# A small tile placed elsewhere, two weight splits queued later, three PSUM adds done after the products

## The chip, the core and the metric

The kernel runs on one core of a Trainium2 chip. A core has five engines with a queue each: TensorE (PE in the profile) multiplies matrices and writes to PSUM, VectorE (DVE) and ScalarE (ACT) do elementwise work, GpSimd (POOL) and SyncE (SP) here issue most of the DMAs, and POOL does a little elementwise work. Each engine works off its own queue and waits for the others by semaphores. The metric is device time in microseconds (us) of one execution; lower is better.

## The reference

One layer over 1024 latent tokens of 1024 channels and 256 context tokens, in fp32:

```
hx = rmsnorm(x) * (1 + sc1) + sh1
z  = hx @ w_in                      -> u_pool, u_lru, u_gate, g_pool, g_lru
m  = sigmoid(g_pool) * (pool_mixer(u_pool) @ w_proj_pool)
   + sigmoid(g_lru)  * (((h_f + h_b) * gelu(u_gate)) @ w_proj_lru)   # h_f, h_b: two RG-LRU scans
x  = x + ga1 * rmsnorm(m @ w_out)
h  = rmsnorm(x) * (1 + sc2) + sh2
g, u = split(h @ w_up)              # 3072 channels each
g  = depthwise 3x3 convolution of g over the 16 x 64 grid + bias
x  = x + ga2 * rmsnorm((gelu(g) * u) @ w_down)
```

## The kernel before, in words

**Arithmetic.** Operands of a matmul are fp32r. To keep fp32 accuracy, each operand is split (function `split`, lines 86 to 88) into a high part, a cast on ScalarE in line 87, and a low part, a subtraction on VectorE in line 88; a product is three matmuls, high by high, high by low and low by high. Nearly every matmul is 128x128 weights by 512 moving columns.

**Order of the work.** First the modulation vectors, then the projections of `hx` by `w_in` (lines 231 to 243, function `unit_mm`), with the pooling branch (lines 303 to 384) and the recurrent units (lines 466 to 534), then the two merging projections and `w_out` (line 702, eight token tiles), then the ConvFFN's up projection (lines 771 to 866, 24 tiles of 128 channels, called f) and the down projection (line 915). An operation can be pulled ahead of its place in the code: the scheduler that builds the queues takes what is ready by priority, and `tc.high_priority(offset=n)` moves an instruction n places ahead. `tc.issue_after(i)` puts every instruction of its block behind instruction i in the queue of i's engine. Tiles that share a tag share its buffers: a new tile's first writer waits until all readers of the tile that had the buffer are done, and buffers are handed out in the order of the code.

**Memory.** The pools lie one behind the other: `cpool`, `gpool`, `small`, then `hp` (the tiles `hx`, `hy`, `h2` under one tag) and the pools of the stages. A tile takes a multiple of 32 bytes of each partition. In the built program, `gpool`'s buffers start at multiples of 64 bytes: `raw` at 15296, 19392 and 23488, `whl`, the split weights, at 27584, 35776 and 43968. The last tile of `small` is `s2l`, 8 bytes at 55232, so `hp` starts at 55264, which is 32 modulo 64, and all tiles of `hp` and of the stages' pools that matmuls read (`hx`, `hy`, `yps`, `h2`, `nf`, `wf`, `w22`, `wd`, `gt`) start at 32 modulo 64. So `whl` meets operands at another place, and the others meet operands at their own. In the profile the weights of line 702 and of the recurrent units also bear the name `whl`, but lie in a stage's pool, at 32.

**The ConvFFN up projection.** It computes each tile's two 1024-token halves as a 2x2 block product by seven products of blocks (Winograd's form of Strassen's method) instead of eight. The activation forms are made once. `h2` holds four blocks and two of their differences, made in `h2_tile` (lines 657 to 676) from each token tile's transposes (line 661). `nf` (lines 752 to 765) holds three more forms: N2 is `n2raw`, N3 and N4 are sums of it with blocks of `h2`, made in two tiles `nt` (lines 763 and 764) and split by `nsplit` (lines 754 to 757), each in two halves. The tiles `nt` have the tag `gc` with two buffers, as have the tiles `gc` of the tiles f, which hold the convolution's input in the left half and its result in the right half.

For the first three tiles (f < NPF = 3), the weight forms were made earlier and are loaded from DRAM on POOL's queue, and the two products with the plain weights `whl` were done between the token tiles (loop in lines 740 to 745): one on X (right half of the PSUM tile `XQ`), one on Q (its left half). For f >= 3 `weights(f)` (lines 769 to 792) loads two weight tiles on SP's queue into `raw` (three buffers), splits them (`load_pair`, lines 678 to 684, with priority WPRI = 200) and makes four sums and three more splits on VectorE and ScalarE.

A tile f has `mid` and `tail`. In `mid` (lines 808 to 834), for the first three tiles, the first product on X is saved by `fork` (a copy on ScalarE into a tile `fk`, line 797), the product with N2 is added on X, the one with N3 starts `v`, X is copied again, and line 829 adds the saved product to Q on VectorE. Then come the product with N1 on X and a third copy. For f >= 3 the saved product is copied to Q itself (line 818) and PE adds to it there. In `tail` (lines 836 to 866) X gets the product with B22 and `v` the one with N4; line 843 subtracts, line 845 starts the convolution's result on ScalarE with the middle tap, and eight more taps follow in line 856 on VectorE; GELU is line 864, the product with u line 865, the store line 866 on POOL's queue.

`s2l` itself is used once, in the last row tile of the down projection (function `finish`), for two partial sums of squares.

Of the kernel before, what the change touches and what calls it, by code (L numbers as in the profile page):

```python
# [8 lines left out]
F32 = mybir.dt.float32  # L9
# [8 lines left out]
P = 128  # L18
# [22 lines left out]
def block_kernel(ctx: ExitStack, tc: tile.TileContext, x, cx, vecs, rowv, icnt, w_mod1, w_mod, w_in, pool_w,  # L41
# [41 lines left out]
    def f32(ap):  # L83
        return ap.bitcast(F32)
# [468 lines left out]
    with tc.tile_pool(name="pj", bufs=1, reuse_waits="tile") as zp:  # L553
# [121 lines left out]
            A.copy(hi, n1)  # L675
            V.tensor_sub(lo, n1, f32(hi))

        def load_pair(f):
            ru = gpool.tile([P, 1024], F32, name=uid("raw"), tag="raw", bufs=3)
            nc.sync.dma_start(ru, w_up[NF + f])  # L680
            w = gpool.tile([P, 2, 1024], F32R, name=uid("whl"), tag="whl", bufs=3)
            with tc.high_priority(offset=WPRI):
                split(w[:, 0, :], w[:, 1, :], ru)
            return ru, w

# [63 lines left out]
    with tc.tile_pool(name="ff", bufs=1, reuse_waits="tile") as zp:  # L749
# [3 lines left out]

        def nsplit(q, src):
            for a in range(0, 4, 2):
                A.copy(nf[:, q, a:a + 2, 0, :], src[:, a:a + 2, :])
                V.tensor_sub(nf[:, q, a:a + 2, 1, :], src[:, a:a + 2, :], f32(nf[:, q, a:a + 2, 0, :]))  # L757

        nsplit(0, n2raw)
        for q, o in ((1, 0), (2, 4)):  # L760
            t = zp.tile([P, 4, 512], F32, name=uid("nt"), tag="gc", bufs=2)
            for a in range(0, 4, 2):
                V.tensor_add(t[:, a:a + 2, :], n2raw[:, a:a + 2, :], f32(h2[:, 0, o + a:o + a + 2, 0, :]))  # L763
                V.tensor_add(t[:, a:a + 2, :], t[:, a:a + 2, :], f32(h2[:, 0, o + a:o + a + 2, 1, :]))  # L764
            nsplit(q, t)

        pairs = {}

        def weights(f):
            w22 = zp.tile([P, 2, 512], F32R, name=uid("w22"), tag="w22", bufs=2)  # L770
            w2 = zp.tile([P, 2, 1024], F32R, name=uid("wf"), tag="wf", bufs=3)
            w3 = zp.tile([P, 2, 1024], F32R, name=uid("wf"), tag="wf", bufs=3)
            L, R = slice(0, 512), slice(512, 1024)
            if f < NPF:
                w1 = wu[f][1]
                G.dma_start(w3, wf_d[f, 1])
                G.dma_start(w2, wf_d[f, 0])
                G.dma_start(w22, w22_d[f])
                pairs[f] = (lh(w1, 0), lh(w1, 1), lh(w22, 0), lh(w2, 1), lh(w3, 0), lh(w2, 0), lh(w3, 1))
                return  # L780
            ru, w1 = load_pair(f)
            rg = gpool.tile([P, 1024], F32, name=uid("raw"), tag="raw", bufs=3)
            nc.sync.dma_start(rg, w_up[f])
            with tc.high_priority(offset=WPRI):
                split(w22[:, 0, :], w22[:, 1, :], rg[:, R])
                V.tensor_add(rg[:, R], rg[:, L], rg[:, R])
                V.tensor_add(rg[:, L], rg[:, L], ru[:, L])
                V.tensor_add(ru[:, L], ru[:, L], rg[:, R])
                V.tensor_add(ru[:, R], ru[:, R], ru[:, L])
                split(w2[:, 0, :], w2[:, 1, :], rg)  # L790
                split(w3[:, 0, :], w3[:, 1, :], ru)
            pairs[f] = (lh(w1, 0), lh(w1, 1), lh(w22, 0), lh(w2, 1), lh(w3, 0), lh(w2, 0), lh(w3, 1))

        def fork(src):
            t = zp.tile([P, 512], F32, name=uid("fk"), tag="fk", bufs=3)
            with tc.high_priority(offset=FPRI):
                A.copy(t, src)  # L797
            return t
# [9 lines left out]
        def mid(f):  # L808
            a11, a12, a22, s1, s2, s3, s4 = pairs[f]
            xq, v = XQ[f % 3], Vps[:, (f % 2) * 512:(f % 2 + 1) * 512]  # L810
            X, Q = xq[:, 512:1024], xq[:, 0:512]
            gc = zp.tile([P, 2, SEQ], F32, name=uid("gc"), tag="gc", bufs=2)
            first = f < NPF
            if first:
                p1 = fork(X)
            else:
                with tc.high_priority(offset=FPRI):
                    A.copy(Q, X)
            if f == 0:
                prod(X, s2, N2, False)  # L820
                prod(v, s3, N3, True)
            else:
                prod(v, s3, N3, True)
                prod(X, s2, N2, False)
            u2 = fork(X)
            if not first:
                prod(Q, a12, B21, False)
            if first:
                V.tensor_add(Q, Q, p1)  # L829
            prod(X, s1, N1, False)  # L830
            u4 = fork(X)
            with tc.high_priority(offset=FPRI):
                V.tensor_sub(gc[:, 0, 512:1024], v, u4)
            st[f] = (gc, u2)

        def tail(f):
# [4 lines left out]
            prod(v, a22, N4, False)  # L841
            with tc.high_priority(offset=FPRI):
                V.tensor_sub(gc[:, 0, 0:512], v, u2)
            cw = lambda i, j: vcol("ffn_conv_w", (i * 3 + j) * NF + f)
            A.activation(gc[:, 1, :], gc[:, 0, :], AF.Identity, scale=cw(1, 1), bias=vcol("ffn_conv_b", f))  # L845
            gv = gc[:, 0, :].rearrange("p (r w) -> p r w", w=COLS)
# [48 lines left out]
    with tc.tile_pool(name="dn", bufs=1, reuse_waits="tile") as zp:  # L895
# [23 lines left out]
        def finish(h, t):  # L919
# [5 lines left out]
            ss = small.tile([P, 1], F32, name=uid("ss"), tag="ss1", bufs=3)  # L925
            n = 512 if tt == 7 else D
            if tt == 7:
                s2 = small.tile([P, 2], F32, name="s2l", tag="s2l")
                for c in range(2):
                    o = slice(c * 512, (c + 1) * 512)  # L930
                    A.activation(jk[:, o], psd[t][:, o], AF.Square, accum_out=s2[:, c:c + 1])
# [99 lines left out]
```

## Time and profile before

| what | value |
|---|---|
| median of 3 runs | 1673.47 us (1673.36 to 1674.98) |
| the profiled execution, its own time | 1673.71 us |
| its span, first to last instruction | 1671.9 us |
| PE, DVE, ACT, POOL busy | 1612.0, 1161.9, 669.5, 150.4 us |
| mean granted TensorE clock | 0.989 |

The page of the profile gives busy times, the chain of work that ended last and the costliest groups of instructions; the trace can be asked for stretches of time, for lines of the code and for waits. Times of rows count from the span's start. A matmul's length in a row includes the time until its last result is out, some 390 ns, while the next one begins earlier; how fast matmuls follow each other is read from their starts. A wait in brackets is idle time of the engine just before the instruction, and what ended it.

### The profile page before, as it was taken

Reading aid. Unit: us, or ns where it says so; the run is one execution under the profiler, and the core shown is the slowest. Engines: PE = TensorE matmul, PEld = TensorE weight load, DVE = VectorE, ACT = ScalarE, POOL = GpSimd, SP = SyncE. Lnnn points to the kernel's source line nnn. Section 1 sums busy time; section 2 is a strip of 40 time slices with the busy share of each in tenths; the row PEclk is TensorE's granted clock in tenths of the full one; section 3 lists DMA queues with packets and bytes.
Section 4 is the critical chain, followed back from the end, with each engine's and each line's share of the span. In section 5 each row is a group of like instructions: output and inputs, shape, how many; then the busy total and the mean of one; then the engine's idle time right before and its main releaser. Section 6 shows DMA issues by size and latency. Waiting matters only on the chain.

```text
span 1671.9 us, 18190 instructions
## 1 busy us (share of the span) xinstructions
PE 1612.0 (96%) x7120; PEld 1292.9 (77%) x7120; DVE 1161.9 (69%) x1290; ACT 669.5 (40%) x801; POOL 150.4 (9%) x208
## 2 busy tenths in 40 slices
PE   6899999999999999999999699999999998999997
PEld 4588877877778788888788478888888886888886
DVE  7777673787887744355387689999999998436323
ACT  8523322655577543122143233334333343425222
POOL 1300200111112220010111000000000000000000
PEclk9999999999999999999999899999999999999999
DMA  8335354424232285588354322222222225845611
GB/s 314 116 92 169 127 187 140 127 83 151 76 128 89 86 283 173 174 272 275 117 157 168 116 88 79 85 76 88 84 80 79 86 66 193 295 141 188 207 57 51
DMA packets 68980, 232.51 MB, mean 139 GB/s; under 512 B 7607, under 2 KB 7735, under 8 KB 68126
## 3 DMA queue, kind: packets, MB, share of 16 engines
q1 hardware_dynamic: 48830, 161.20, 30.2%
q0 software_dynamic: 20064, 70.15, 11.6%
q8 instruction: 56, 0.92, 0.2%
q14 instruction: 30, 0.25, 0.0%
HBM read 177.30 MB, written 54.02 MB: 138 GB/s over the span
## 4 chain that ended last, share of the span: by engine, by line
PE 41%; DVE 6%; DMA 2%; issue 1%; ACT 1%; DVEq 0%; POOL 0%; ACTq 0%; SPq 0%; POOLq 0%
PE pb L736 10%; PE pb L915 8%; PE pc L736 6%; PE pd L736 5%; PE pb L702 5%; PE pd L915 4%; PE pc L915 4%; DVE gc L856 2%; DMA raw<-in_w_up_dram 1%; DVE wf L88 1%; DVE nf L757 0%; ACT whl L87 0%; DVE gc L865 0%; DVE nt L764 0%; DVE nt L763 0%
## 5 line engine op out<-in xcount | busy, mean ns | idle before, releaser
L241 PE MATMUL pu<-hx,whl 128*128 128x512 f32 x1056 | 270.5, 396 | 1.3 <-DVE whl L88 1.3
L856 DVE SCALAR_TENSOR_TENSOR gc<-gc,vec 128x945 f32<-128x945 f32 (+1 forms) x192 | 234.5, 1221 | 6.5 <-ACT gc L845 2.2
L241 PEld LDWEIGHTS pu<-hx,whl 128*128 128x128 f32 x1056 | 185.8, 188 | 43.6 <-DVE whl L88 1.9
L87 ACT CAST whl<-raw 128x1024 fp32r<-128x1024 f32 (+1 forms) x98 | 99.3, 1014 | 294.7 <-PE pu L241 62.6
L88 DVE TENSOR_TENSOR whl<-raw,whl 128x1024 fp32r<-128x1024 f32 (+1 forms) x98 | 116.9, 1195 | 89.3 <-ACT whl L87 87.4
L915 PE MATMUL pb<-wd,gt 128*128 128x512 f32 x552 | 132.2, 392 | 0.0
L88 DVE TENSOR_TENSOR wd<-rw,wd 128x1024 fp32r<-128x1024 f32 x46 | 56.3, 1223 | 98.0 <-ACT wd L87 98.0
L915 PEld LDWEIGHTS pb<-wd,gt 128*128 128x128 f32 x552 | 104.6, 190 | 21.9
L241 PE MATMUL pg<-hx,whl 128*128 128x512 f32 x480 | 119.0, 400 | 0.0
L241 PEld LDWEIGHTS pg<-hx,whl 128*128 128x128 f32 x480 | 89.3, 190 | 21.1
L736 PE MATMUL pb<-h,wf 128*128 128x512 f32 x384 | 93.1, 391 | 4.3 <-DVE pb L829 3.0
L736 PE MATMUL pb<-h,whl 128*128 128x512 f32 x384 | 96.4, 395 | 0.7 <-ACT fk L797 0.7
L87 ACT CAST wf<-raw 128x1024 fp32r<-128x1024 f32 x42 | 44.0, 1048 | 120.8 <-PE pb L736 77.8
L87 ACT CAST wd<-rw 128x1024 fp32r<-128x1024 f32 x46 | 48.4, 1053 | 109.5 <-PE pc L915 100.8
L241 PE MATMUL pb<-hy,whl 128*128 128x512 f32 x384 | 90.4, 395 | 0.0
L702 PE MATMUL pb<-whl,mH 128*128 128x512 f32 x384 | 89.1, 391 | 0.6 <-ACT mH L696 0.6
L736 PEld LDWEIGHTS pb<-h,wf 128*128 128x128 f32 x384 | 71.5, 188 | 21.6 <-DVE pb L829 3.8
L736 PEld LDWEIGHTS pb<-h,whl 128*128 128x128 f32 x384 | 71.8, 187 | 18.5 <-ACT fk L797 1.4
L241 PEld LDWEIGHTS pb<-hy,whl 128*128 128x128 f32 x384 | 72.0, 187 | 17.6
L702 PEld LDWEIGHTS pb<-whl,mH 128*128 128x128 f32 x384 | 71.5, 188 | 16.3 <-ACT mH L696 1.1
L736 PE MATMUL pc<-nf,wf 128*128 128x512 f32 x288 | 71.7, 396 | 2.1 <-DVE nf L757 2.0
L915 PE MATMUL pd<-wd,gt 128*128 128x512 f32 x276 | 69.4, 392 | 3.8 <-ACT gt L87 3.5
(276 smaller groups left out, 2830.4 us busy)
## 6 DMA issues: line engine op xcount, KB each, us to landing
raw<-in_w_up_dram SPq DMA_DIRECT2D x51, 512.0 KB, 3.6
rw<-in_w_down_dram SPq DMA_DIRECT2D x46, 512.0 KB, 4.6
raw<-in_w_in_dram SPq DMA_DIRECT2D x40, 512.0 KB, 4.6
rawm<-in_w_mod_dram SPq DMA_DIRECT2D x32, 512.0 KB, 4.2
gu_d<-gc POOLq DMA_DIRECT2D x24, 512.0 KB, 2.9
rg<-gu_d SPq DMA_DIRECT2D x46, 256.0 KB, 4.7
w<-in_w_mod_dram SPq DMA_DIRECT2D x16, 512.0 KB, 6.5
sg_d<-sg POOLq DMA_DIRECT2D x16, 512.0 KB, 3.6
```

The source lines that it names most:

```text
L87: A.copy(hi, src)
L88: V.tensor_sub(lo, src, f32(hi))
L241: mm = T.matmul(ps[:, h * 512:(h + 1) * 512], wv[:, wi, k, :], act(h, k, ai), start=st, stop=sp)
L702: mm = T.matmul(ps[:, h * 512:(h + 1) * 512], mh[ai][:, k, :], wo[k][:, wi, h * 512:(h + 1) * 512], start=(k == 0 and i == 0), stop=(k == ...
L736: mm = T.matmul(ps, w(wi, j), b(ai, j), start=(start and j == 0 and i == 0), stop=(j == 3 and i == 2), skip_group_check=True)
L856: V.scalar_tensor_tensor(o, gv[:, r0 + dr:r1 + dr, c0 + dc:c1 + dc], cw(i, j), o, op0=ALU.mult, op1=ALU.add)
L915: T.matmul(psd[t][:, c * 512:(c + 1) * 512], gt[:, ai, t * P:(t + 1) * P], wd[:, wi, c * 512:(c + 1) * 512], start=(f == 0 and i == 0), st ...
```

## The change

`s2l` moves from `small` to the pool of the down projection (named `dn`), and gets 64 bytes. The split in `load_pair` is put behind the last two instructions of the last `nsplit` for f = 3 and f = 4. For the first three tiles the saved product is copied to the right half of `gc` instead of an `fk` tile, and its addition to Q comes after the last product of the tile, just ahead of line 845 (numbers of the kernel before), which overwrites that half.

```diff
--- before.py
+++ after.py
@@ -675,11 +675,14 @@
             A.copy(hi, n1)
             V.tensor_sub(lo, n1, f32(hi))
 
-        def load_pair(f):
+        def load_pair(f, after=()):
             ru = gpool.tile([P, 1024], F32, name=uid("raw"), tag="raw", bufs=3)
             nc.sync.dma_start(ru, w_up[NF + f])
             w = gpool.tile([P, 2, 1024], F32R, name=uid("whl"), tag="whl", bufs=3)
-            with tc.high_priority(offset=WPRI):
+            with ExitStack() as es:
+                for i in after:
+                    es.enter_context(tc.issue_after(i.ins))
+                es.enter_context(tc.high_priority(offset=WPRI))
                 split(w[:, 0, :], w[:, 1, :], ru)
             return ru, w
 
@@ -753,8 +756,9 @@
 
         def nsplit(q, src):
             for a in range(0, 4, 2):
-                A.copy(nf[:, q, a:a + 2, 0, :], src[:, a:a + 2, :])
-                V.tensor_sub(nf[:, q, a:a + 2, 1, :], src[:, a:a + 2, :], f32(nf[:, q, a:a + 2, 0, :]))
+                ca = A.copy(nf[:, q, a:a + 2, 0, :], src[:, a:a + 2, :])
+                cv = V.tensor_sub(nf[:, q, a:a + 2, 1, :], src[:, a:a + 2, :], f32(nf[:, q, a:a + 2, 0, :]))
+            return ca, cv
 
         nsplit(0, n2raw)
         for q, o in ((1, 0), (2, 4)):
@@ -762,7 +766,7 @@
             for a in range(0, 4, 2):
                 V.tensor_add(t[:, a:a + 2, :], n2raw[:, a:a + 2, :], f32(h2[:, 0, o + a:o + a + 2, 0, :]))
                 V.tensor_add(t[:, a:a + 2, :], t[:, a:a + 2, :], f32(h2[:, 0, o + a:o + a + 2, 1, :]))
-            nsplit(q, t)
+            nsp = nsplit(q, t)
 
         pairs = {}
 
@@ -778,7 +782,7 @@
                 G.dma_start(w22, w22_d[f])
                 pairs[f] = (lh(w1, 0), lh(w1, 1), lh(w22, 0), lh(w2, 1), lh(w3, 0), lh(w2, 0), lh(w3, 1))
                 return
-            ru, w1 = load_pair(f)
+            ru, w1 = load_pair(f, nsp if f < NPF + 2 else ())
             rg = gpool.tile([P, 1024], F32, name=uid("raw"), tag="raw", bufs=3)
             nc.sync.dma_start(rg, w_up[f])
             with tc.high_priority(offset=WPRI):
@@ -812,7 +816,8 @@
             gc = zp.tile([P, 2, SEQ], F32, name=uid("gc"), tag="gc", bufs=2)
             first = f < NPF
             if first:
-                p1 = fork(X)
+                with tc.high_priority(offset=FPRI):
+                    A.copy(gc[:, 1, 0:512], X)
             else:
                 with tc.high_priority(offset=FPRI):
                     A.copy(Q, X)
@@ -825,8 +830,6 @@
             u2 = fork(X)
             if not first:
                 prod(Q, a12, B21, False)
-            if first:
-                V.tensor_add(Q, Q, p1)
             prod(X, s1, N1, False)
             u4 = fork(X)
             with tc.high_priority(offset=FPRI):
@@ -841,6 +844,9 @@
             prod(v, a22, N4, False)
             with tc.high_priority(offset=FPRI):
                 V.tensor_sub(gc[:, 0, 0:512], v, u2)
+            if f < NPF:
+                with tc.high_priority(offset=FPRI):
+                    V.tensor_add(xq[:, 0:512], xq[:, 0:512], gc[:, 1, 0:512])
             cw = lambda i, j: vcol("ffn_conv_w", (i * 3 + j) * NF + f)
             A.activation(gc[:, 1, :], gc[:, 0, :], AF.Identity, scale=cw(1, 1), bias=vcol("ffn_conv_b", f))
             gv = gc[:, 0, :].rearrange("p (r w) -> p r w", w=COLS)
@@ -925,7 +931,7 @@
             ss = small.tile([P, 1], F32, name=uid("ss"), tag="ss1", bufs=3)
             n = 512 if tt == 7 else D
             if tt == 7:
-                s2 = small.tile([P, 2], F32, name="s2l", tag="s2l")
+                s2 = zp.tile([P, 16], F32, name="s2l", tag="s2l")
                 for c in range(2):
                     o = slice(c * 512, (c + 1) * 512)
                     A.activation(jk[:, o], psd[t][:, o], AF.Square, accum_out=s2[:, c:c + 1])
```

## Rows read from the trace of the kernel before

**Rows 1.** The page, part 1: busy time and share of the span of each engine.

```profile
PE 1612.0 (96%) x7120; PEld 1292.9 (77%) x7120; DVE 1161.9 (69%) x1290; ACT 669.5 (40%) x801; POOL 150.4 (9%) x208
```

**Rows 2.** Stretches of the span: length, then busy time (instructions) of PE, PEld, DVE, ACT, POOL.

```profile
72.00:366.00 294.00, 293.88 (x1302) 235.55 (x1303) 197.19 (x182) 107.63 (x120) 34.39 (x62) 1.00 0.41 132
366.00:562.00 196.00, 187.16 (x865) 150.56 (x863) 162.37 (x133) 123.63 (x121) 33.19 (x22) 0.97 0.35 112
...
1005.00:1380.00 375.00, 374.92 (x1630) 304.07 (x1629) 359.09 (x368) 144.99 (x175) 10.69 (x20) 1.00 0.25 81
```

**Rows 3.** Three of these stretches, instructions of line 241 alone.

```profile
72.00:366.00 294.00, 245.72 (x1009) 184.42 (x1009) 1.00 0.41 132
366.00:562.00 196.00, 141.45 (x526) 90.13 (x524) 0.97 0.35 112
562.00:805.00 243.00, 241.49 (x1035) 193.92 (x1035) 1.00 0.66 219
```

**Rows 4.** Timeline of PE in the projections: start, length, instruction, count.

```profile
642.15 11.36 PE L241 MATMUL pd<-yps,whl 128*128 128x512 f32 x48
653.35 9.03 PE L241 MATMUL pc<-yps,whl 128*128 128x512 f32 x38
```

**Rows 5.** The chain that ended last, in the down projection: start, length, count.

```profile
1507.99 16.32 PE pb L915 x72
```

**Rows 6.** Timeline of PE, first matmuls of the down projection.

```profile
1396.74 2.96 PE L915 MATMUL pb<-whl,w 128*128 128x512 f32 x12
1399.54 1.56 PE L915 MATMUL pc<-whl,w 128*128 128x512 f32 x6
```

**Rows 7.** Groups of instructions: shapes, count, busy time, mean ns, idle before.

```profile
L241 PE MATMUL pb<-hy,whl 128*128 128x512 f32 x384 | 90.4, 395 | 0.0
...
L702 PE MATMUL pb<-whl,mH 128*128 128x512 f32 x384 | 89.1, 391 | 0.6 <-ACT mH L696 0.6
...
L497 PE MATMUL pg<-xp,whl 128*128 128x512 f32 x192 | 61.2, 415 | 7.5 <-ACT i L503 7.5
```

**Rows 8.** Who waited for whom on DVE, 1010 to 1380 us: total, times, longest.

```profile
DVE whl L88 <- ACT whl L87: 8.2, 17, 0.6
...
DVE gc L843 <- PE pc L736: 0.7, 1, 0.7
```

**Rows 9.** Timeline of DVE, one round of the ConvFFN.

```profile
1105.79 1.23 DVE L88 TENSOR_TENSOR whl<-raw,whl 128x1024 fp32r<-128x1024 f32 x1 [0.49 <-ACT whl L87]
...
1119.14 1.22 DVE L88 TENSOR_TENSOR wf<-raw,wf 128x1024 fp32r<-128x1024 f32 x1
...
1125.03 1.23 DVE L88 TENSOR_TENSOR whl<-raw,whl 128x1024 fp32r<-128x1024 f32 x1 [0.47 <-ACT whl L87]
```

**Rows 10.** Timeline of ACT and DVE around the activation forms.

```profile
921.06 1.05 ACT L87 CAST whl<-raw 128x1024 fp32r<-128x1024 f32 x1 [6.42 <-DMA raw<-in_w_up_dram]
...
922.14 1.22 DVE L88 TENSOR_TENSOR whl<-raw,whl 128x1024 fp32r<-128x1024 f32 x1 [5.03 <-ACT whl L87]
...
936.68 1.22 DVE L757 TENSOR_TENSOR nf<-nt,nf 128x1024 fp32r<-128x1024 f32 x1
...
941.22 0.69 DVE L829 TENSOR_TENSOR pd<-pd,fk 128x512 f32<-128x512 f32 x1
942.41 1.23 DVE L757 TENSOR_TENSOR nf<-nt,nf 128x1024 fp32r<-128x1024 f32 x1 [0.50 <-ACT nf L756]
...
955.99 1.20 DVE L856 SCALAR_TENSOR_TENSOR gc<-gc,vec 128x945 f32<-128x945 f32 x1 [1.38 <-ACT gc L845]
```

**Rows 11.** Timeline of PE in the same stretch.

```profile
916.89 1.04 PE L661 MATMUL pc<-ident,xo 128*128 128x128 f32 x8
...
927.02 0.71 PE L736 MATMUL pd<-nf,wf 128*128 128x512 f32 x1 [4.44 <-ACT nf L756]
...
941.97 5.49 PE L736 MATMUL pd<-h,wf 128*128 128x512 f32 x12 [2.60 <-DVE pd L829]
```

**Rows 12.** The stretch 930 to 944 us, columns as in group 2, then the granted clock.

```profile
930.00:944.00 14.00, 9.35 (x27) 6.43 (x26) 13.14 (x12) 4.74 (x5) 0.00 (x0) 0.74 0.00 1
```

## The prediction

> **What bounds the kernel now.** I read the totals first. TensorE (PE below) is busy for 96% of the span [rows 1], so the question for each stretch is whether PE runs without a hole there, and how fast. From 72 to 366 us and from 562 to 805 us it does: 293.88 of 294 us and 241.49 of 243 us [rows 2, 3]. From 366 to 562 us, the recurrent units, it is idle for 8.8 us [rows 2], and one wait explains most of that: line 497 waits 7.5 us for ScalarE to empty its PSUM tile [rows 7]. From 1005 to 1380 us, the ConvFFN, PE is busy for 374.92 of 375 us but VectorE (DVE) for 359.09 as well [rows 2]; which of the two sets the pace there has to be worked out below.
>
> Next I read how fast matmuls of one shape (128x512, fp32r) follow each other. In line 241, 48 of them take 653.35 - 642.15 = 11.20 us, 233.3 ns each [rows 4]. In line 915, 72 take 16.32 us, 226.7 ns each [rows 5]. What differs is the place of the two operands modulo 64 bytes: `whl` starts at 0 and `yps` at 32, while `wd` and `gt` both start at 32. Line 915's own first matmuls, whose moving operand is a `whl` at 0 and whose weights are a tile at 32, run at (1399.54 - 1396.74) / 12 = 233.3 ns [rows 6], so it is not the line. The output projection (line 702) has both operands at 32 and a mean length of 391 ns; line 241 with `hy` at 32 and `whl` at 0 has 395 [rows 7]. So one place is worth 233.3 - 226.7 = 6.67 ns per matmul, before any theory of why.
>
> **The moved tile.** In the built program it takes 32 bytes at the end of `small`. Without it everything behind `small` starts 32 bytes earlier: at 0 modulo 64, where `whl` and `raw` are already. Every pair of operands then has one place. No row shows two operands at 0; the nearest are the pairs at 32, and I take 226.7 ns for it.
>
> The gain counts only where PE is what the stretch waits for. Line 241 has 1009 matmuls from 72 to 366 us and 1035 from 562 to 805 us [rows 3]: 2044 x 6.67 ns = **13.6 us**. The few matmuls of 256 columns between them are left out. In the recurrent units 526 x 6.67 = 3.5 us is the most; part of it will only lengthen the wait for ScalarE. PE is full for all but 8.8 of the 196 us, so I take two thirds, 2.3 us, and keep 0 and 3.5. The short groups of lines 376 and 497 have both operands at 32 and are still slow: mean 415 ns in line 497 [rows 7] against 391, the stall in it included. They stand between `whl` matmuls, and I read this as a pace that needs some matmuls to settle. If it then need not, 288 x 6.67 = 1.9 us is the most (192 and, by the loops, 96 matmuls); I take 1.0, keeping 0 and 1.9. Sum of 13.6, 2.3 and 1.0: **16.9 us**.
>
> In the ConvFFN a tile f has 84 matmuls, 24 with `whl`. PE needs 24 x 233.3 + 60 x 226.7 ns = 19.20 us for them, afterwards 84 x 226.7 = 19.04. But DVE has a round of its own: the split of `whl` at 1105.79, DVE work without a hole until the second `wf` split ends at 1120.36 and frees a `raw` buffer, then the next load and its cast, then the next `whl` split at 1125.03 [rows 9]. That is 19.24 us, with 0.47 us of idle in it that belongs to the load; in 370 us DVE waits only 0.7 us for PE [rows 8]. So DVE sets this pace, and the 0.16 us per tile that PE gains turn into idle time: I take 0, and 20 x 0.16 = 3.2 us as the other end. The 48 `whl` matmuls at the start of the down projection gain 0.3 us ahead of a wait for loads: 0. The 64 bytes in `dn` cost nothing; the tile has the same writers.
>
> Here a page speaks against the change. The Trainium skill, "SBUF — State Buffer" (SBUF: two separate sides), says that PE, ACT and DVE's own ports never wait on anyone, and gives PE two independent read ports; by it both places would run alike, and this part would be worth 0 us. The trace disagrees: 226.7 against 233.3 ns in the same line [rows 5, 6].
>
> **The two splits.** ScalarE's cast of the fifth tile's weights sits in its queue from 914.6 to 921.06, 6.42 us, waiting for its load; DVE's half of the split, at 922.14, waits 5.03 us for it [rows 10]. Behind both stand the forms of the last token tile, whose transposes ended at 917.93 [rows 11]. With the splits behind the last `nf` form, those start at about 918.0 and not after the split's 1.15 us, at 923.3: the chain of `nt` and `nf` forms on DVE moves 5.3 us earlier. Its last form ran to 943.64; it will run to about 937.7 (0.6 us more, since the add of line 829 leaves the chain). The splits, 2 x 1.05 us on ScalarE and 2 x 1.15 on DVE, follow there in a hole: between 943.64 and 955.99 DVE does two short subtractions. No load moves on SP's queue or POOL's: the issues stand outside the block, and the `raw` buffers are held until the weight sums anyway.
>
> **The adds and the copy.** PE waited 2.60 us for the first add of line 829 [rows 11] and less for the other two; these waits go. But the saved product now goes to the right half of `gc`, not to `fk`, and `gc` shares its two buffers with the two `nt` tiles. So the first copy must wait until the first `nt` is used up, its last form ending at 937.90 [rows 10], 932.6 in the new order, and the product on X, which overwrites what is copied and began at 927.02 [rows 11], cannot start before 933.2. What is late next is this product. In the meantime PE can do N3's 12 matmuls, whose last operand is ready at 932.6: until about 934. Then X by N2 (12 x 226.7 = 2.7 us, or 5.1 at the lower clock, the 5.49 below less the last matmul's end), a copy (0.7, as line 829's add of as many columns), N1 (2.7), a copy (0.7), B22 (2.7), N4 (2.7), then two DVE operations of 0.69 and the 1.38 for the form on ScalarE: the first of the nine-tap operations at 949 to 952, against 955.99 [rows 10]. That is 4 to 7 us. The clock matters: its mean from 930 to 944 us was 0.74, so part of that at 1.2 GHz [rows 12], after PE had stood idle for 4.44 us, and 12 matmuls that began at 941.97 took 5.49 us [rows 11]; the new order has an equal hole. I take **5 us**. At worst the forms do not move and the copy waits for 937.9: 1.3 us lost. At best the copy costs nothing: 5.0 us of DVE wait and some 7 of the 11 us of DVE idle between 943.64 and 955.99 (12.35 less two subtractions of 0.69), 12 us gained. From then on DVE has work without a stop, so whatever is won stays won. The third tile's copy waits likewise for the store of the first tile's result; DVE's queue sets the pace there, so 0. The adds themselves are three on DVE either way, now ahead of ScalarE's form in line 845: 0.6 us each in that chain, counted above for the first.
>
> **Sum.** 16.9 + 5 = 21.9 us. The profiled execution took 1673.71 us around its span of 1671.9, 0.24 above the median of 1673.47; from the former 1651.8, from the median **1651.6 us**. Ends: 13.6 - 1.3 = 12.3 us (1661), and 13.6 + 3.5 + 1.9 + 3.2 + 12 = 34.2 (1639).
>
> **Rivals.** First, place makes no difference: the 6.67 ns belong to the buffers that are refilled beside the matmuls. For it: `whl` is always such a buffer. Against it: `wf`, `wd` and `gt` are refilled too, and line 915's `whl` was complete. Then only the 5 us remain: 1668.5. 6%. The page of the Trainium skill named above would give this too.
>
> Second, and slower: the cost is not a difference of places but an operand at 0. Each slow pair has exactly one such operand, each fast one none, and after the move all have two. Then line 241 stays at 233.3 and the others join it: 1104 matmuls of line 915 by its loops (7.4 us), 384 of line 702 (2.6), and in the ConvFFN 84 x 233.3 = 19.60 us against DVE's 19.24, 20 x 0.36 = 7.2. 17.2 less the 5 us is 12.2 us slower: 1685.7. It decides from about 231 ns per pair at 0, where what line 241 still gains is what the others lose. Against it: slow is the case with the moving operand at 0 as much as with the weights at 0, which looks like a relation. 7%.
>
> Third, the copy's wait eats the transition whole and the recurrent units absorb the rest: 1661, still faster. 17%.
>
> **Numbers.** My forecast has 70%. A measurement of this kernel can tell about 0.2%, 3.3 us, from no change. The forecast and the third rival are faster by more; of the first rival's 6% I put half within it, since its 5 us may shrink: faster 0.90, within it 0.03, slower 0.07. The range from 1640 to 1664 leaves out the first two rivals and a few per cent more.
>
> **What would show it.** Right: 226.7 ns in line 241, with the lengths of line 915 unchanged; a ConvFFN round still of 19.24 us with more DVE wait for `whl` or PE holes; the last token tile's forms at once behind their transposes; no PE wait for DVE in the three early tiles, and a copy on ScalarE just behind the first `nt` tile's last form. Wrong: 233 ns anywhere at two operands of one place, or a ConvFFN round that shortens with PE.

## The result, and the profile after

The changed kernel takes 1656.88 us (median of 4 runs, 1656.34 to 1657.70) against 1673.41 us before (4 runs): 16.5 us less, ratio 0.990 with a 95% interval from 0.9883 to 0.9917. The forecast was 1651.6 us within 1640 to 1664: right in direction and range, and 5.3 us too fast. The profiled execution took 1656.47 us around a span of 1654.7 us, 17.2 us under the span before.

The page, part 1, of the changed kernel answers to [rows 1]:

```profile
PE 1593.4 (96%) x7120; PEld 1290.3 (78%) x7120; DVE 1160.5 (70%) x1290; ACT 669.1 (40%) x801; POOL 150.2 (9%) x208
```

TensorE has the same 7120 matmuls and 18.6 us less busy time; VectorE, ScalarE and POOL have the same as before to within 1.5 us. So the gain is in TensorE's pace, or in its waits. The timeline of PE in the projections answers to [rows 4], and the chain of waits in the down projection to [rows 5]:

```profile
635.99 11.04 PE L241 MATMUL pd<-yps,whl 128*128 128x512 f32 x48
646.87 11.04 PE L241 MATMUL pc<-yps,whl 128*128 128x512 f32 x48
```

```profile
1490.75 16.32 PE pb L921 x72
```

In line 241, 48 matmuls now take 646.87 - 635.99 = 10.88 us, 226.7 ns each instead of 233.3. The down projection (now line 921) keeps its 16.32 us. Now the same line over two stretches that end where the work does, other than in [rows 3]: the windows view for the instructions of line 241 alone, length and then PE busy (count), first the kernel before and then the changed one.

```profile
277.00:366.00 89.00, 64.98 (x244) 41.16 (x244) 1.00 0.37 119
...
564.00:805.00 241.00, 241.00 (x1034) 193.61 (x1033) 1.00 0.66 220
```

```profile
271.00:361.00 90.00, 65.55 (x247) 41.60 (x245) 1.00 0.36 117
...
560.00:795.00 235.00, 235.00 (x1038) 194.53 (x1037) 1.00 0.67 226
```

In the second stretch, the projections, one matmul costs 235.00 / 1038 = 226.4 ns of busy time instead of 241.00 / 1034 = 233.1. In the first, ahead of the recurrent units, it is 65.55 / 247 = 265.4 after 266.3: almost nothing. There and in the recurrent units line 241 mostly does not run in long rows. For half of its matmuls (386 of the 770 from 277 to 562 us) one of 256 columns comes after every two of 512 (line 243, and line 499 behind 497 in the same way); the other half, those of the gates, run in pieces of 5 to 27 and one of 48. Five such groups of three in either kernel, from the timeline of PE, first before and then after:

```profile
375.77 0.62 PE L241 MATMUL pu<-hx,whl 128*128 128x512 f32 x2
...
378.67 0.63 PE L241 MATMUL pu<-hx,whl 128*128 128x512 f32 x2
```

```profile
370.51 0.63 PE L241 MATMUL pu<-hx,whl 128*128 128x512 f32 x2
...
373.44 0.63 PE L241 MATMUL pu<-hx,whl 128*128 128x512 f32 x2
```

2.90 us before and 2.93 after, so 580 and 586 ns per group: the place bought nothing here. The gates' 384 matmuls did gain a little, 94.1 us of busy time after 96.3. The next table follows single instructions through both traces and books what is won between them; the two late tanh forms are those that stand behind a cast waiting for its load, and that PE waits for.

| instruction | before | after | won so far |
|---|---|---|---|
| row of six matmuls of line 234 | 60.45 | 59.91 | 0.5 |
| column sums, line 269 | 276.70 | 271.43 | 5.3 |
| first late tanh form, line 503 | 391.23 | 385.95 | 5.3 |
| second late tanh form, line 503 | 429.73 | 424.60 | 5.1 |
| first matmul on `pb` in line 241 | 563.64 | 559.69 | 4.0 |
| output projection, line 702 (705) | 810.96 | 800.49 | 10.5 |
| last transposes, line 661 | 916.89 | 905.68 | 11.2 |
| first nine-tap operation, line 856 (862) | 955.99 | 939.44 | 16.6 |
| last `whl` split of the ConvFFN, line 88 | 1367.24 | 1350.36 | 16.9 |
| end of the span | 1671.9 | 1654.7 | 17.2 |

The gain comes in three pieces: 4.7 us up to 277 us, 6.5 us in the projections, 5.3 us in the transition. The recurrent units give 1.3 us back. The next rows, of ScalarE, VectorE and PE in the changed kernel's transition, answer to [rows 10, 11].

```profile
910.56 1.22 DVE L767 TENSOR_TENSOR nt<-n2raw,h 128x1024 f32<-128x1024 f32 x1
...
920.77 1.23 DVE L760 TENSOR_TENSOR nf<-nt,nf 128x1024 fp32r<-128x1024 f32 x1
...
926.52 1.23 DVE L760 TENSOR_TENSOR nf<-nt,nf 128x1024 fp32r<-128x1024 f32 x1 [1.12 <-ACT nf L759]
927.66 1.22 DVE L88 TENSOR_TENSOR whl<-raw,whl 128x1024 fp32r<-128x1024 f32 x1
...
939.44 7.54 DVE L862 SCALAR_TENSOR_TENSOR gc<-gc,vec 128x945 f32<-128x945 f32 x6 [1.31 <-ACT gc L851]
```

```profile
922.03 0.59 ACT L820 COPY gc<-pd 128x512 f32<-128x512 f32 x1
```

```profile
916.32 0.63 PE L739 MATMUL pc<-nf,wf 128*128 128x512 f32 x1 [4.55 <-ACT nf L759]
...
923.61 2.93 PE L739 MATMUL pd<-nf,wf 128*128 128x512 f32 x12
```

The forms follow behind the transposes with no split between, and the splits have moved behind the last form. The copy waits until the first `nt` tile is used up (920.77 + 1.23 = 922.00), and the product on X starts behind it, at 923.61. TensorE does N3's product before.

### The profile page after: what moved, and what is told of

Read it like the earlier page. It is cut to its first block, busy times and chain, and to the rows that moved or that the text cites. A ratio compares the mean times of both kernels' runs of the same rounds, so it can differ in the third digit from the quotient of the medians.

```text
span 1654.7 us, 18184 instructions
## 1 busy us (share of the span) xinstructions
PE 1593.4 (96%) x7120; PEld 1290.3 (78%) x7120; DVE 1160.5 (70%) x1290; ACT 669.1 (40%) x801; POOL 150.2 (9%) x208
## 4 chain that ended last, share of the span: by engine, by line
PE 31%; DVE 15%; DMA 3%; ACT 2%; issue 1%; DVEq 0%; ACTq 0%
PE pb L921 8%; DVE gc L862 6%; PE pb L705 5%; PE pb L739 5%; PE pd L921 4%; PE pc L921 4%; DMA raw<-in_w_up_dram 3%; PE pc L739 3%; PE pd L739 2%; DVE wf L88 2%; DVE gc L871 1%; ACT whl L87 1%; DVE whl L88 1%; DVE gc L846 1%; DVE raw L792 1%
## 5 line engine op out<-in xcount | busy, mean ns | idle before, releaser
L241 PE MATMUL pu<-hx,whl 128*128 128x512 f32 x1056 | 266.7, 392 | 1.4 <-DVE whl L88 1.0
L921 PEld LDWEIGHTS pb<-wd,gt 128*128 128x128 f32 x552 | 104.5, 189 | 21.9
L739 PEld LDWEIGHTS pc<-nf,wf 128*128 128x128 f32 x288 | 53.7, 192 | 27.6 <-DVE gc L846 8.5
```

The lines of the kernel that those rows point to most:

```text
L241: mm = T.matmul(ps[:, h * 512:(h + 1) * 512], wv[:, wi, k, :], act(h, k, ai), start=st, stop=sp)
L739: mm = T.matmul(ps, w(wi, j), b(ai, j), start=(start and j == 0 and i == 0), stop=(j == 3 and i == 2), skip_group_check=True)
L921: T.matmul(psd[t][:, c * 512:(c + 1) * 512], gt[:, ai, t * P:(t + 1) * P], wd[:, wi, c * 512:(c + 1) * 512], start=(f == 0 and i == 0), st ...
```

## The experiments

All ratios compare with the kernel before, run beside them on the same chip (median 1674.72 us for the first four runs, 1673.82 for the next four, 1674.43 for the last three). Differences to the changed kernel use its 1656.88 us from above, beside which the kernel before took 1673.41; they can be off by the 0.4 to 1.0 us between these medians.

**One: is it the place?** The tile stays in `small` and is made longer, so that only the addresses behind it move:

```
-                s2 = small.tile([P, 2], F32, name="s2l", tag="s2l")
+                s2 = small.tile([P, 16], F32, name="s2l", tag="s2l")
```

> The kernel before, in which the 8-byte tile stays in `small` but is made 64 bytes long, so that all behind it moves by 32 bytes and nothing else changes. Theory (place modulo 64 bytes): line 241 at 226.7 ns outside the recurrent units, and the time falls by 10 to 11.5 us, to 1662 to 1663.5, as the changed kernel had gained 10.8 us by 911 us. Rival (leaving `small`, or the tile's other writers, is what counts): 233.3 ns and 1673. Rival (the recurrent units lost 2 us in the changed kernel by chance of the clock): 1659 to 1661.

Measured: 1667.19 us, ratio 0.9954 (0.9942 to 0.9967), about 7.5 us faster and not 10 to 11.5. The timeline of PE shows why:

```profile
638.16 11.15 PE L241 MATMUL pd<-yps,whl 128*128 128x512 f32 x48
649.15 11.15 PE L241 MATMUL pc<-yps,whl 128*128 128x512 f32 x48
```

(649.15 - 638.16) / 48 = 229.0 ns, neither of the two paces seen so far. So an address alone changes the pace, and nothing else has to move: the first rival falls. The second had 1659 to 1661 us, which did not come either. The pace accounts for the miss: 4.3 of the 6.67 ns are won, and about as large a share of the 10 to 11.5 us. So two operands at the same place modulo 64 are not enough for the fast pace, and the theory's modulus is wrong.

**Two, three and four: the parts of the transition.** The splits alone:

```
-            ru, w1 = load_pair(f)
+            ru, w1 = load_pair(f, nsp if f < NPF + 2 else ())
```

(with `load_pair` and `nsplit` as in the change); the copy and the late adds alone:

```
-                p1 = fork(X)
+                with tc.high_priority(offset=FPRI):
+                    A.copy(gc[:, 1, 0:512], X)
...
-            if first:
-                V.tensor_add(Q, Q, p1)
...
+            if f < NPF:
+                with tc.high_priority(offset=FPRI):
+                    V.tensor_add(xq[:, 0:512], xq[:, 0:512], gc[:, 1, 0:512])
```

and both of these, without the moved tile (from the changed kernel):

```
-                s2 = zp.tile([P, 16], F32, name="s2l", tag="s2l")
+                s2 = small.tile([P, 2], F32, name="s2l", tag="s2l")
```

> The kernel before with the two splits queued behind the last nf form, nothing else. Theory (the chain of nt and nf forms on VectorE decides the transition): the forms of the last token tile start 5.3 us earlier against their transposes, and the time falls by 4 to 5.5 us, to 1668 to 1669.5, since the add of line 829 still stands in the chain. Rival (the copy and the late add bring the 5.8 us that the transition gained, the splits little): within 1.5 us of 1673.5.

> The kernel before with the saved product in the right half of gc and its add behind the products, nothing else. Theory: the split of the fifth tile still holds the forms of the last token tile back, and the copy of the first saved product now waits for the last form of the first nt tile, so only the 0.6 us of the add in the chain and the waits for it go: 0.5 to 1.5 us faster, 1672 to 1673. Rival (the waits of TensorE for the adds, 2.60 and 2.16 and 0.83 us, are what went): 4 to 5.6 us faster.

> The changed kernel with its tile back in `small`, 8 bytes long: the splits, the copy and the late adds without the place. Theory (two parts that add up): 5 to 6 us faster than before, 1667.5 to 1668.5, with line 241 at 233.3 ns as before, and a ConvFFN round of the same length. Rival (the place also buys time in the transition or in the ConvFFN, so that the parts do not add up): over 3 us away from that.

Measured: the splits alone 1668.30 us, ratio 0.9964 (0.9951 to 0.9976); the adds alone 1674.44 us, 0.9999 (0.9990 to 1.0008); both 1668.54 us, 0.9966 (0.9954 to 0.9978). The first nine-tap operation starts at 950.21, 957.11 and 950.06 us, against 955.99 before. So the splits are the whole of the transition's gain, and the copy with the late adds is worth nothing, less even than the little expected. Its rows on ScalarE and PE, in the run of the adds alone, show what it trades:

```profile
940.21 0.59 ACT L816 COPY gc<-pd 128x512 f32<-128x512 f32 x1
```

```profile
934.49 0.80 PE L736 MATMUL pc<-nf,wf 128*128 128x512 f32 x1 [10.65 <-ACT nf L756]
...
941.96 2.94 PE L736 MATMUL pd<-nf,wf 128*128 128x512 f32 x12
```

The wait of 2.60 us for the add is gone [rows 11], but the product on X, which began at 927.02 before [rows 11], begins at 941.96, behind the copy.

**Five: the copy's buffer.** The changed kernel with the saved products in a buffer of their own, 2 KB per partition:

```
-                    A.copy(gc[:, 1, 0:512], X)
+                    p1 = zp.tile([P, 512], F32, name=uid("p1"), tag="p1", bufs=1)
+                    A.copy(p1, X)
...
-                    V.tensor_add(xq[:, 0:512], xq[:, 0:512], gc[:, 1, 0:512])
+                    V.tensor_add(xq[:, 0:512], xq[:, 0:512], p1)
```

> The changed kernel with the first saved products copied into a buffer of their own instead of the right half of gc. Theory (the copy at 922.03 us waits for the last form of the first nt tile, and the product on X waits for the copy): the copy moves to about 911 us, the X product starts with the first nf form at about 916 us, the five products of f = 0 (2.7 us each, some of it at 1.2 GHz) end by 931 to 935, and the first nine-tap operation comes 3 to 6 us before its 939.44; as VectorE has work from there on without a stop, the kernel is 3 to 6 us faster than the changed one: 1651 to 1654. Rival (the chain of nt and nf forms alone sets the end of the transition): first nine-tap operation still at 938 to 940, no gain.

Measured: 1648.01 us, ratio 0.9845 (0.9830 to 0.9860), 8.9 us under the changed kernel's 1656.88. The timelines of ScalarE, PE and VectorE:

```profile
903.46 0.58 ACT L821 COPY p<-pd 128x512 f32<-128x512 f32 x1
```

```profile
911.62 0.39 PE L739 MATMUL pd<-nf,wf 128*128 128x512 f32 x1
```

```profile
932.71 7.54 DVE L863 SCALAR_TENSOR_TENSOR gc<-gc,vec 128x945 f32<-128x945 f32 x6 [1.38 <-ACT gc L852]
```

The transposes ended at the same time as in the changed kernel (905.70 and 905.68). The copy no longer waits, the X product starts 12 us earlier, and the nine-tap work 939.44 - 932.71 = 6.7 us earlier. The theory holds, and more than the 3 to 6 us expected is won. Of the 8.9 us, 6.7 are there at the first nine-tap operation; at the fourth tile's product with u the lead is 1012.75 - 1003.43 = 9.3 us, and where these last two came from was not traced. Part of the surplus may be the clock, in the windows view (PEclk is the column behind POOL), first the changed kernel and then this run:

```profile
903.00:940.00 37.00, 28.64 (x119) 22.17 (x118) 26.71 (x29) 13.24 (x16) 3.18 (x6) 0.91 0.51 185
```

```profile
903.00:940.00 37.00, 32.85 (x140) 24.85 (x139) 33.00 (x34) 14.33 (x18) 3.70 (x7) 1.00 0.53 196
```

The granted clock stays at its full level of 2.4 GHz, where the changed kernel, after PE had stood idle for 4.55 us, had a part at 1.2 GHz (mean 0.91). How much of the time that is worth was not tried by itself.

**Six: the groups of three.** The 256-column matmuls of a recurrent unit behind its 512-column ones, in lines 241 with 243 (shown), and line 499 in the same way in a loop of its own behind 497:

```
-                if extra is not None:
-                    mm = T.matmul(extra[0], wv[:, wi, k, :], extra[1](k, ai), start=st, stop=sp)
+        if extra is not None:
+            for k in range(KT):
+                for i, (wi, ai) in enumerate(((0, 0), (0, 1), (1, 0))):
+                    mm = T.matmul(extra[0], wv[:, wi, k, :], extra[1](k, ai),
+                                  start=(k == 0 and i == 0), stop=(k == KT - 1 and i == 2))
```

> The changed kernel with the 256-column matmuls of the recurrent units issued behind the 512-column ones of their unit instead of one after every two. Theory (operands of one place give 226.7 ns only in unbroken rows of 512 columns; the 256-column matmuls between keep the others at 231 to 233): the 512-column matmuls of lines 241 and 497 there fall from 231.1 and 232.5 to about 227 ns, up to 2.9 us of matmul time between 271 and 560 us; up to the second stall the loop of VectorE, ScalarE and loads swallows most, so 0.5 to 2 us faster than the changed kernel. Rival (the refill of buffers beside the matmuls slows them): lengths stay at 231 to 233 ns.

Measured: 1665.46 us, ratio 0.9945 (0.9930 to 0.9960): 8.6 us slower than the changed kernel. In line 241 the pace did what the theory says, though not from the start of a row; in line 500 (497 before) it did not (PE):

```profile
279.67 11.09 PE L241 MATMUL pu<-hx,whl 128*128 128x512 f32 x48
...
307.25 1.55 PE L500 MATMUL pg<-xp,whl 128*128 128x512 f32 x6
308.63 0.52 PE L503 MATMUL pc<-xp,whl 128*128 128x256 f32 x3
```

```profile
281.75 9.01 PE L241 MATMUL pu<-hx,whl 128*128 128x512 f32 x39
290.59 3.04 PE L245 MATMUL pc<-hc,whl 128*128 128x256 f32 x24
```

The second view starts inside the row of 48 matmuls that the first shows whole. Its first nine take 281.75 - 279.67 = 2.08 us, 231.1 ns each, and the other 39 take 290.59 - 281.75 = 8.84 us, 226.7 ns each. Line 500's rows of six are over before that: 308.63 - 307.25 = 1.38 us, 230.0 ns each, though its operands, too, are at one place. So the pace needs some matmuls to settle. Besides, the order of the queues changed, and PE stood before the first projection until ScalarE had emptied the gate's tile:

```profile
564.03 4.16 PE L241 MATMUL pb<-hx,whl 128*128 128x512 f32 x9 [8.26 <-ACT sg L466]
```

So the expected length was right for line 241 in the main, wrong for line 497, and the expected time was wrong: here the waits weigh more than the pace. From the column sums to the first projection PE is busy for 272.35 us instead of 277.19, and idle for 19.7 instead of 11.8 (windows 272 to 564 us here, 271 to 560 in the changed kernel).

**Seven: the first stall.** The tanh forms of the recurrent units at a higher priority, so that ScalarE does the first late form ahead of a weight cast:

```
-    TPRI, SPRI, ALT = 100, 0, ((0, 2), (1, 2))
+    TPRI, SPRI, ALT = 300, 0, ((0, 2), (1, 2))
```

> The changed kernel with the tanh forms of the recurrent units at a higher priority, so that in the first stall (387 us) ScalarE does them ahead of a weight cast that waits for its load. Theory (the stalls at 387 and 425 us come from a cast that waits for its load at the head of ScalarE's queue): the stall of 4.2 us at 387 us goes, 3 to 4 us less there; the second stall depends on the loop of 38.5 us from one form to the next, so the gain holds only if that loop starts earlier too: 0 to 4 us faster than the changed kernel. Rival (the weights are needed that early, so TensorE waits for them instead): no gain or up to 3 us slower.

Measured: 1651.80 us, ratio 0.9869 (0.9853 to 0.9886), 5.1 us under the changed kernel, somewhat more than expected. The timeline of ScalarE, first the changed kernel and then this run:

```profile
385.00 1.04 ACT L87 CAST whl<-raw 128x1024 fp32r<-128x1024 f32 x1 [4.24 <-DMA raw<-in_w_in_dram]
385.95 1.11 ACT L503 ACTIVATE i<-pg,vec 128x1024 f32<-128x1024 f32 x1
...
424.60 1.09 ACT L503 ACTIVATE i<-pg,vec 128x1024 f32<-128x1024 f32 x1
```

```profile
382.05 1.12 ACT L503 ACTIVATE i<-pg,vec 128x1024 f32<-128x1024 f32 x1
...
420.40 1.09 ACT L503 ACTIVATE i<-pg,vec 128x1024 f32<-128x1024 f32 x1
```

From the first form to the second it is 38.65 us in the changed kernel, 38.35 here, and 38.50 before (429.73 - 391.23). That time did not follow TensorE's pace, which is one in the kernel before and another in these two; when the first form comes 3.9 us earlier, so does the second (4.2). Waits are not all that went. In these units PE is idle for 8.7 us instead of 11.8, and its work itself takes 273.28 us instead of 277.19 at a mean granted clock of 1.00 instead of 0.98 (windows 272 to 554 us here, 271 to 560 in the changed kernel).

**Eight and nine: which modulus?** The kernel before with a tile of 128 or 256 bytes in `small`, and a tile of 64 or 128 bytes between `wd` and `gt` in the down projection:

```
-                s2 = small.tile([P, 2], F32, name="s2l", tag="s2l")
+                s2 = small.tile([P, 32], F32, name="s2l", tag="s2l")
...
+            if not padded:
+                padded.append(zp.tile([P, 16], F32, name="pad", tag="pad"))
```

> The kernel before, with the tile in `small` 128 bytes long, so that the moving operand of line 241 stands 128 bytes behind the weights modulo 512, and with 64 bytes between wd and gt, so that in line 915 it stands 64 bytes ahead of the weights. If the place counts modulo 64 bytes: 226.7 ns in both. If it counts modulo 128: 226.7 in line 241 and 233.3 in line 915 (as its whl matmuls at that distance, 448 modulo 512, have in the run with the long tile). If modulo 512: neither at 226.7.

> The kernel before, with the tile in `small` 256 bytes long (line 241: moving operand 256 bytes from the weights modulo 512) and 128 bytes between wd and gt (line 915: moving operand 128 bytes ahead of the weights, 384 modulo 512). So far the distance modulo 512 and the pace were: 0 and 226.7 ns, 32 and 233.3, 64 and 228.9, 128 and 232.4, 448 and 233.3, 480 and 233.3. If the distance counts modulo 256: 226.7 in line 241. If modulo 512, the step of the weights from one matmul pair to the next: another pace, 228 to 234. Line 915: above 230 by either.

The timeline of PE for line 241, and the chain of waits for the down projection (there line 917), first the run with 128 bytes, then that with 256:

```profile
630.28 11.32 PE L241 MATMUL pc<-yps,whl 128*128 128x512 f32 x48
641.44 11.31 PE L241 MATMUL pd<-yps,whl 128*128 128x512 f32 x48
```

```profile
1418.56 2.80 PE pb L917 x12
```

```profile
636.38 11.04 PE L241 MATMUL pd<-yps,whl 128*128 128x512 f32 x48
647.26 11.04 PE L241 MATMUL pc<-yps,whl 128*128 128x512 f32 x48
```

```profile
1410.15 2.79 PE pb L917 x12
```

(641.44 - 630.28) / 48 = 232.5 ns and (647.26 - 636.38) / 48 = 226.7; 2.80 / 12 = 233.3 and 2.79 / 12 = 232.5 in the down projection. With the addresses of the built programs (`whl` starts at byte 27584 of a partition in all of them, and `yps` lies as `hx` does), the pace goes by the distance from the weights to the moving operand:

| kernel, line | moving tile | distance mod 256 | ns per matmul |
|---|---|---|---|
| changed, 241 | `hx` at 55232 | 0 | 226.7 |
| 256-byte tile, 241 | `hx` at 55488 | 0 | 226.7 |
| before, 241 | `hx` at 55264 | 32 | 233.3 |
| 64-byte tile, 241 | `hx` at 55296 | 64 | 229.0 |
| 128-byte tile, 241 | `hx` at 55360 | 128 | 232.5 |
| 256-byte tile, 917 | 128 bytes ahead of the weights | 128 | 232.5 |
| 128-byte tile, 917 | 64 bytes ahead of the weights | 192 | 233.3 |
| before, 915 with `whl` moving | 32 bytes ahead of the weights | 224 | 233.3 |

Modulo 64 and modulo 128 are both out: 64 and 128 apart would have been the fast place. Modulo 256 fits every row. The two runs took 1679.94 and 1670.41 us (one run each): the slower down projection costs the first more than line 241 saves.

**Ten and eleven: versions that beat both kernels.** The buffer of run five and the priority of run seven together; and, on top, the reordering of run six for lines 241 and 243 alone.

> The changed kernel with both: the buffer of their own for the saved products, and the higher priority of the tanh forms. Theory (the two gains, 8.9 us at the transition and 5.1 us at the first stall, lie in stages that follow each other, so they add up): 1642 to 1645. Rival (one eats the other): 1647 to 1650.

> As the run with both, and in the input products of the recurrent units (line 241 with line 243) the 256-column matmuls behind all 512-column ones. Theory (512-column matmuls in unbroken rows at one place: 226.7 instead of 231 ns): line 241 there at 227 ns, 1 to 1.5 us less matmul time before the stalls and as much behind them, 0 to 2.5 us faster than the run with both. Rival (the order in which ScalarE and the loads are queued decides, as in the run in which all units were reordered and a stall of 8.65 us came up at 555 us): slower by 1 to 8 us.

Measured: both together 1642.08 us, ratio 0.9807 (0.9793 to 0.9821), 14.8 us under the changed kernel's median, where the two alone gave 8.9 and 5.1, so 14.0: they add up. With the reordering 1649.28 us, 0.9849 (0.9835 to 0.9863), so 7.2 us slower again: its rival was right. The windows view of the recurrent units, and line 497 in the groups view of PE (line 500 there), first the run with both and then that with the reordering:

```profile
272.00:553.00 281.00, 274.11 (x1285) 221.02 (x1283) 224.78 (x189) 173.99 (x173) 45.49 (x33) 0.99 0.36 116
```

```profile
L497 PE MATMUL pg<-xp,whl 128*128 128x512 f32 x192 | 59.8, 408 | 3.8 <-ACT r L503 2.3 <-ACT i L503 1.4
```

```profile
272.00:560.50 288.50, 274.80 (x1288) 223.03 (x1286) 227.52 (x191) 182.85 (x180) 51.13 (x35) 0.98 0.37 116
```

```profile
L500 PE MATMUL pg<-xp,whl 128*128 128x512 f32 x192 | 60.3, 412 | 6.8 <-ACT i L506 6.8
```

PE's work is no shorter (274.80 us after 274.11), and PE is idle for 288.50 - 274.80 = 13.7 us instead of 6.9. The wait of line 497 for the tanh form `i` is back among that, 6.8 us after 1.4.

## Why the prediction was right, and where its sizes were off

Right: the place in the projections, the splits, the copy's wait, the ConvFFN. Wrong: the recurrent units and the stretch ahead of them, and the modulus. Part of the closeness is luck: the misses of 1.6 and 4.6 us there are met by 1.8 us in the rest, for which the sum had nothing and which the runs do not explain.

| step | forecast, us | measured, us |
|---|---|---|
| line 241, 72 to 277 us (765 x 6.67 ns) | 5.1 | 4.7 |
| line 241, 277 to 366 us (244 x 6.67 ns) | 1.6 | 0.0 |
| recurrent units, and lines 376 and 497 | 3.3 | -1.3 |
| line 241, 562 to 805 us (1035 x 6.67 ns) | 6.9 | 6.5 |
| transition | 5.0 | 5.3 |
| the rest (start 0.5, output projection 0.7, ConvFFN 0.3, end 0.3) | 0 | 1.8 |
| sum | 21.9 | 17.0 |

The measured column comes from the table of instructions above; its sum is the span's 17.2 but for rounding. The medians differ by 16.5.

**The moved tile.** "226.7 ns in line 241" came true where the 512-column matmuls follow each other without a break. The failed step is that each of the 2044 matmuls of line 241, and each of the 526 in the recurrent units, was priced at 6.67 ns. The prediction left out "the few matmuls of 256 columns". But they decide the pace of the others. In a group of two and one the pace is 580 to 586 ns at either place, and run six shows that the same line returns to 226.7 ns in an unbroken row, after the first nine matmuls at 231.1. So of the forecast 16.9 us, some 5 were not there to be had.

**The recurrent units** were taken as PE time with a wait that absorbs a third. They behave like a loop of ScalarE, VectorE and loads, 38.4 to 38.7 us from one late form to the next in three kernels, and what PE gains inside is lost in the wait at its end: line 497 waits 8.6 us for form `i` in the changed kernel, after 7.5 [rows 7]. The 1.0 us for lines 376 and 497 fell for two other reasons, both visible now. Line 497's 512-column matmuls run in groups with line 499, and line 376's operands are at a distance of 128 modulo 256, in both kernels. Reading these groups as "a pace that needs some matmuls to settle" was right for line 497, as run six shows; what failed is the 1.0 us taken for its no longer having to, since it still has to with both operands at one place. For line 376 the modulus of 64 hid the distance. Of the 1.3 us lost, 1.2 went between the second late form and 564 us. The windows view, from the two late forms on, first before and then after, shows what differs there:

```profile
391.00:401.00 10.00, 8.61 (x29) 7.05 (x30) 5.43 (x5) 7.98 (x10) 2.31 (x1) 0.66 0.25 79
429.00:439.00 10.00, 8.12 (x31) 6.66 (x32) 7.16 (x8) 8.20 (x10) 2.90 (x1) 0.83 0.45 152
```

```profile
385.70:395.70 10.00, 8.59 (x33) 7.11 (x34) 5.69 (x5) 8.45 (x11) 2.31 (x1) 0.83 0.27 78
424.60:434.60 10.00, 8.85 (x29) 7.25 (x30) 6.35 (x7) 6.97 (x9) 2.89 (x1) 0.66 0.43 143
```

After each stall the granted clock is low for a while, 0.66 and 0.83 on average, and the longer of the two stretches changed sides: as I read it, what that gave after the first stall went into the wait for the second form, and what it cost after the second stayed. These lengths differ from one profiled run to the next, in runs of either place, so nothing shows this part to be an effect of the change.

**The transition.** The forecast of 5 us and of a first nine-tap operation at 949 to 952 us holds: with everything ahead unchanged it was 950.06 us. The splits' 5.3 us are the gain (run two). The copy waits for the first `nt` tile as predicted, its last form ending at 922.00 us, which with the 11.2 us won ahead of it is 933.2 in the time of before, for a forecast of 932.6. The prediction counted the copy as a delay inside the 5 us. Run five shows that this delay was worth 8.9 us, more than the splits gained; the prediction's own best case, 12 us against 5, had put it at 7.

**The ConvFFN** was to keep its round of 19.24 us, as VectorE sets it. The timeline of DVE in the changed kernel, beside [rows 9]:

```profile
1088.97 1.23 DVE L88 TENSOR_TENSOR whl<-raw,whl 128x1024 fp32r<-128x1024 f32 x1 [0.61 <-ACT whl L87]
...
1108.17 1.23 DVE L88 TENSOR_TENSOR whl<-raw,whl 128x1024 fp32r<-128x1024 f32 x1 [0.43 <-ACT whl L87]
```

1108.17 - 1088.97 = 19.20 us, and from the first to the last `whl` split of this stage the lead grows by 0.2 us (974.52 to 1350.36 us after, 991.20 to 1367.24 before). PE now stands idle for 361 - 359.74 = 1.26 us of this stretch (windows 1005 to 1366 us), against 0.08 before [rows 2]; 0.16 us per tile would have been some 3 us. The down projection is unchanged.

**The rivals.** Place as no effect (1668.5 us) and an operand at 0 as the cost (1685.7 us) both fell with the first row of the timeline. The Trainium skill, "SBUF — State Buffer" (SBUF: two separate sides), says that PE never waits on anyone. It speaks of contention between engines. The runs here show one line on the same data at 226.7, 229.0, 232.5 and 233.3 ns by the distance of its operands alone, which does not follow from that section. The third rival, a transition eaten whole and recurrent units that absorb the rest (1661 us), was half right: the units absorbed, and the transition held.

What stays open: why the distance counts, why a row needs some ten matmuls to settle, and whether that is also why a 256-column matmul between undoes the gain. The distances 96 and 160 were not tried. Nor were lines 241 and 497 in unbroken rows without a change in the order of the other queues, so what the pace alone would give there is not measured.

## What to carry to other kernels

Price a faster instruction only in the stretch where it sets the pace, and look at what is interleaved with it: the same matmul gained 6.7 ns in unbroken rows and nothing among shorter ones. When a part of a change helps one wait, look for the buffer it now shares: the late adds were worth nothing until their copy had a buffer of its own, and with the splits that buffer was then worth 8.9 us. Before building on a rule like "the same place modulo 64", try the next multiple, for one kernel with a longer tile was enough to refute it.

## What was not expected of the hardware

The pace of fp32r matmuls of 512 columns, each with its own 128-column weights, goes by the distance of moving operand and weights modulo 256 bytes: 226.7 ns at 0, 229.0 at 64, 232.5 at 128, 233.3 at 32, 192 and 224. This holds in unbroken rows; the first nine of a row at 0 took 231.1 ns each (run six). Matmuls of 256 columns in a row go the other way. Fifteen of them in line 243 take 1.91 us at a distance of 32 and 1.96 at 0 (timeline of PE, before and after); all 192 of the line are busy for 51.6 us before, 52.2 after, and 52.3 with the 256-byte tile, again at 0 (groups view):

```profile
304.90 1.91 PE L243 MATMUL pc<-hc,whl 128*128 128x256 f32 x15
```

```profile
299.63 1.96 PE L243 MATMUL pc<-hc,whl 128*128 128x256 f32 x15
```
